# Row scaling and plain transposes in the norms of a transformer kernel, with split work, bank reads and product order changed at the stage borders

## The chip, the core and the metric

The kernel runs on one core of a Trainium2 chip. The metric is the device time of one execution in microseconds. TensorE multiplies, VectorE (DVE), ScalarE (ACT) and GpSimd (POOL) work on tiles, and SyncE (SP) issues the loads. TensorE writes its results to PSUM, which has eight banks of 512 float32 columns; all other tiles lie in SBUF, 128 rows each.

## What is computed

512 tokens of width 1024 in float32 go through two blocks. Cut to what matters here:

```python
# first block, layers i = 0 (nsa) and 1 (swa); mod = silu(c) @ ada_w[i] + ada_b[i] -> sh1, sc1, g1, sh2, sc2, g2
h = modulate(rms_norm(x, norm_g[i, 0]), sh1, sc1)
y = nsa_mixer(h, ...) if i == 0 else swa_sink_mixer(h, ...)
x = x + (1 + g1) * rms_norm(y, norm_g[i, 1])
h = modulate(rms_norm(x, norm_g[i, 2]), sh2, sc2)
x = x + (1 + g2) * rms_norm(squared_relu_mlp(h, ...), norm_g[i, 3])
# second block
x = x + hybrid_mixer(rms_norm_2(x, norm_mix_w), ...)
x = x + memory_cross_attention(rms_norm_2(x, norm_xattn_w), rms_norm_2(mem, norm_mem_w), ...)
x = x + conv_ffn(rms_norm_2(x, norm_ffn_w), ...)
return rms_norm_2(x, norm_final_w)
```

rms_norm divides each token's row by the root of its mean square and multiplies each column by a gain; modulate multiplies by 1 + scale and adds shift.

## The kernel before

The program is one straight run of stages: nsa, mlp0, swa, mlp1, hybrid, cross, ffn. `x` holds the residual as four tiles of 128 tokens by 1024 columns. What a stage multiplies, `h`, lies the other way round: eight chunks of 128 columns by 512 tokens, each as a high part `hH` and a low part `hL`, so that three products of reduced precision (`mm3`, L124 to L126: high by high, low by high, high by low) stand for one of float32. Weights come in tiles of 512 KB: `wload` loads `st`, ScalarE writes the high part `wh` (L95), and VectorE, or GpSimd where a table says so, writes the low part `wl` (L96). Loads are issued in program order; there are three `st` tiles and five pairs of `wh` and `wl`, and `extra` draws some pairs from another pool.

At a border between stages the last products of the old stage give rows of `y`, by two token tiles and then one and one. VectorE adds them up and multiplies by the gain (L914, or L916 and L918 in the mlps), ScalarE sums squares (L284), `rcol` makes the reciprocal root `rc_r` in four instructions on one column (L275 to L278), L926 adds the rows to `x`, and the same again gives the `rc_r` of the next norm. Then `norm_T` makes `h`: it builds a diagonal matrix of `rc_r` (L291) for each token tile, multiplies each 128 x 128 block of `x` by it on TensorE (L298), which turns the block round and scales it in one, and evacuates the bank: gain and shift into a tile `nt` (L308 on ScalarE and L310 on VectorE, in turn by chunk, so that both read one bank), then the split into `hH` (L95) and `hL` (L96). A norm without a shift (memory, hybrid, cross, ffn) goes from the bank at once to `hH` (L303, ScalarE) and `hL` (L304, VectorE). Behind the border the first weights of the new stage are multiplied with tokens 0 to 255 first, weight by weight, since these are ready first, and then with tokens 256 to 511: `project_halves` in the mlps with seven weights, `project` with `keep=4` in swa, hybrid, cross and ffn. The second half runs over the eight chunks `k` outside and the weights inside, so all its banks end together, each followed by its `evac`.

Besides this, `ada` jobs (L331: a load of 512 KB and one VectorE row that multiplies and sums) make the modulation of the first block; `wload` takes one from a queue for each weight, until the queue is empty. `mem_keys` (128 x 256 products, eight weights) and `mem_values` (eight weights) are work of the cross stage that is put into the borders behind mlp0 and mlp1. A scheduler with a timing model of its own orders the instructions of all engines; each engine then runs its list in order.

Of the kernel before, what the change touches and what calls it, by code (L numbers as in the profile page):

```python
# [21 lines left out]
NB = 'AVAVAVAV'  # L22
# [16 lines left out]
KG, KG4 = (4, 5, 6), (3,)  # L39
# [6 lines left out]
def body(nc, tc, A, out):  # L46
# [114 lines left out]
    def project(srcs, h, evac, keep=0, nk=8, on_pool=()):  # L161
        full = slice(0, 512)
        if keep:
            ws, banks = [], []
            for i in range(keep):
                ws.append(wload(srcs[i], eng=G if i in KG4 else V))
                banks.append(mm())
            for i in range(keep):
                mm3(banks[i][:, HALVES[0]], chunk_terms(ws[i], h, HALVES[0], range(nk)))
            for k in range(nk):  # L170
                for i in range(keep):
                    c = HALVES[1]
                    w = ws[i]
                    mm3(banks[i][:, c], [(kc(w[0], k), kc(w[1], k), h[0][k][:, c], h[1][k][:, c])], start=k == 0,
                        stop=k == nk - 1)
# [110 lines left out]
    def norm_T(xs, Rs, h, c, a, b=None):  # L286

        ds, w = [], 128 * len(xs)
        for r in Rs:
            d = tmp("diag", [128, 128], bufs=4)  # L290
            V.tensor_scalar(d, ident, r, None, op0=OP.mult)  # L291
            ds.append(d)
        nb = 512 // w
        for m0 in range(0, 8, nb):
            o = mm("t")
            for u in range(nb):
                for i, x in enumerate(xs):
                    T.matmul(o[:, u * w + i * 128:u * w + i * 128 + 128], kc(x, m0 + u), ds[i], start=True, stop=True)  # L298
            for u in range(nb):
                m = m0 + u  # L300
                hh, hl, v, g = h[0][m][:, c], h[1][m][:, c], kc(o, u, w), a[:, m:m + 1]
                if b is None:
                    S.activation(hh, v, AF.Copy, scale=g)  # L303
                    V.scalar_tensor_tensor(hl, v, g, f(hh), op0=OP.mult, op1=OP.subtract)  # L304
                else:
                    t = tmp("nt", [128, 256], bufs=3)[:, :w]
                    if NB[m] == "A":
                        S.activation(t, v, AF.Identity, bias=b[:, m:m + 1], scale=g)  # L308
                    else:
                        V.tensor_scalar(t, v, g, b[:, m:m + 1], op0=OP.mult, op1=OP.add)  # L310
                    split(hh, hl, t)
# [1294 lines left out]
```

## Time and profile before

| | |
|---|---|
| median of 3 runs | 2126.13 us (2123.41 to 2127.01) |
| profiled execution | 2125.28 us, its span 2123.2 us |
| TensorE busy | 2035.6 us, 96% of the span |
| VectorE busy | 1161.2 us, 55% |
| ScalarE busy | 905.3 us, 43% |
| GpSimd busy | 306.4 us, 14% |
| mean granted clock of TensorE | 0.975 |
| chain that ended last | TensorE 86%, VectorE 6%, ScalarE 3%, DMA 3% |

A matmul's length in the profile contains its way through the array, so that neighbours overlap; the pace is the distance from start to start. The chain of the last line is followed back from the end: at each step to what released the instruction. A wait is put down to the engine whose signal came last.

### The profile page before, as it was taken

The numbers are of one execution on the slowest core, as the hardware profiler recorded it, in microseconds if no ns is written. First come the engines' busy times: TensorE is split into PE (matmuls) and PEld (weight loads), VectorE is DVE, ScalarE is ACT, GpSimd is POOL, SyncE is SP. The second block draws the span as 40 slices with busy tenths as digits, with TensorE's granted clock in tenths as the row PEclk, the third lists the DMA queues.
The fourth block names the chain that finished last, engine by engine and source line by source line (L and its number), as shares of the span: only waits on it lengthen the run. The fifth ranks groups of instructions, "written<-read, shape, count | busy, mean of one in ns | idle before, by whom it ended". The sixth has DMA issues, their size and how long they took to land.

```text
span 2123.2 us, 27619 instructions
## 1 busy us (share of the span) xinstructions
PE 2035.6 (96%) x10326; PEld 1666.9 (79%) x10326; DVE 1161.2 (55%) x2322; ACT 905.3 (43%) x1740; POOL 306.4 (14%) x243
## 2 busy tenths in 40 slices
PE   8989999979999999799899999999999999999998
PEld 7766565778888888667788888878888888888886
DVE  7778776455556547584632333465635445445354
ACT  5356565443423236364633232453545444324233
POOL 0401121021201114310121020132010000001000
PEclk8989999999999999899899999999999999999999
DMA  7765331235557534340123233332323122323321
GB/s 292 215 211 149 96 111 48 89 130 203 183 190 228 157 111 142 88 112 30 61 99 94 94 99 99 109 105 84 100 70 109 61 82 80 99 91 98 99 93 57
DMA packets 80855, 247.79 MB, mean 117 GB/s; under 512 B 13137, under 2 KB 16145, under 8 KB 80722
## 3 DMA queue, kind: packets, MB, share of 16 engines
q1 hardware_dynamic: 77618, 240.86, 35.7%
q0 software_dynamic: 1248, 2.59, 0.5%
q10 hardware_dynamic: 1856, 2.59, 0.5%
q8 instruction: 81, 1.33, 0.3%
q14 instruction: 52, 0.43, 0.1%
HBM read 222.47 MB, written 5.77 MB: 107 GB/s over the span
## 4 chain that ended last, share of the span: by engine, by line
PE 86%; DVE 6%; ACT 3%; DMA 3%; issue 2%; ACTq 0%; SPq 0%; DVEq 0%; POOL 0%
PE mm L124 18%; PE mm L126 18%; PE mm L125 18%; PE o L124 4%; PE o L125 4%; PE o L126 4%; PE o L748 3%; PE t L433 3%; PE t L298 2%; DMA ad<-in_ada_w_dram 2%; PE t L124 2%; PE t L125 2%; PE t L126 2%; PE mm L732 1%; ACT wh L95 1%
## 5 line engine op out<-in xcount | busy, mean ns | idle before, releaser
L96 DVE TENSOR_TENSOR wl<-st,wh 128x1024 fp32r<-128x1024 f32 x273 | 341.2, 1254 | 455.2 <-ACT wh L95 454.6
L95 ACT ACTIVATE wh<-st 128x1024 fp32r<-128x1024 f32 x307 | 320.8, 1053 | 554.4 <-PE mm L125 248.2
L124 PE MATMUL mm<-hH,wh 128*128 128x512 f32 (+1 forms) x1456 | 523.4, 361 | 25.7 <-ACT wh L95 14.6
L125 PE MATMUL mm<-hL,wh 128*128 128x512 f32 (+1 forms) x1456 | 522.8, 359 | 0.0
L126 PE MATMUL mm<-hH,wl 128*128 128x512 f32 (+1 forms) x1456 | 521.8, 359 | 0.0
L124 PEld LDWEIGHTS mm<-hH,wh 128*128 128x128 f32 x1456 | 279.7, 193 | 66.5 <-ACT wh L95 19.5
L125 PEld LDWEIGHTS mm<-hL,wh 128*128 128x128 f32 x1456 | 280.0, 192 | 39.5 <-issue 1.1
L126 PEld LDWEIGHTS mm<-hH,wl 128*128 128x128 f32 x1456 | 278.9, 192 | 39.0 <-issue 0.2
L957 POOL TENSOR_TENSOR relu<-relu 128x512 f32<-128x512 f32 (+1 forms) x78 | 104.0, 1339 | 580.3 <-ACT relu L956 492.1
L124 PE MATMUL mm<-wh,aH 128*128 128x512 f32 x444 | 173.9, 393 | 3.9 <-ACT aH L95 3.9
L125 PE MATMUL mm<-wl,aH 128*128 128x512 f32 x444 | 174.2, 392 | 0.0
L126 PE MATMUL mm<-wh,aL 128*128 128x512 f32 x444 | 171.9, 392 | 0.0
L331 DVE SCALAR_TENSOR_TENSOR ad<-ad,cs 128x1024 f32<-128x1024 f32 x90 | 116.0, 1293 | 49.1 <-DMA ad<-in_ada_w_dram 48.6
L96 POOL TENSOR_TENSOR wl<-st,wh 128x1024 fp32r<-128x1024 f32 x32 | 78.1, 2455 | 424.6 <-ACT wh L95 420.7
L124 PE MATMUL o<-wh,aH 128*128 128x512 f32 x284 | 113.1, 398 | 4.8 <-DVE y L914 4.8
L125 PE MATMUL o<-wl,aH 128*128 128x512 f32 x284 | 113.0, 398 | 0.0
L126 PE MATMUL o<-wh,aL 128*128 128x512 f32 x284 | 112.2, 395 | 0.0
L124 PEld LDWEIGHTS mm<-wh,aH 128*128 128x128 f32 x444 | 83.5, 188 | 22.2 <-ACT aH L95 4.1
L126 PEld LDWEIGHTS mm<-wh,aL 128*128 128x128 f32 x444 | 83.6, 188 | 18.1
L125 PEld LDWEIGHTS mm<-wl,aH 128*128 128x128 f32 x444 | 83.5, 188 | 17.8
L433 PEld LDWEIGHTS t<-pack,P 128*128 128x128 f32 x436 | 47.1, 141 | 54.9 <-issue 49.9
L737 ACT ACTIVATE P<-P,m 128x128 f32<-128x128 f32 (+3 forms) x128 | 70.9, 556 | 28.3 <-DVE m L735 26.8
(417 smaller groups left out, 3260.0 us busy)
## 6 DMA issues: line engine op xcount, KB each, us to landing
ad<-in_ada_w_dram SPq DMA_DIRECT2D x90, 512.0 KB, 4.4
st<-in_w_up_dram SPq DMA_DIRECT2D x64, 512.0 KB, 3.6
st<-in_w_down_dram SPq DMA_DIRECT2D x64, 512.0 KB, 3.5
st<-in_w_fup_dram SPq DMA_DIRECT2D x44, 512.0 KB, 3.5
st<-in_w_fdown_dram SPq DMA_DIRECT2D x22, 512.0 KB, 3.5
st<-in_w_nsa_dram SPq DMA_DIRECT2D x16, 512.0 KB, 8.0
st<-in_w_hyb_dram SPq DMA_DIRECT2D x12, 512.0 KB, 3.6
st<-in_w_swa_dram SPq DMA_DIRECT2D x10, 512.0 KB, 3.9
```

Of the source, the lines that this page charges most:

```text
L95: S.activation(h, src, AF.Copy)
L96: eng.tensor_tensor(l, src, f(h), op=OP.subtract)
L124: T.matmul(o, ah, bh, start=start and i == 0, stop=False, **kw)
L125: T.matmul(o, ah, bl, start=False, stop=False, **kw)
L126: T.matmul(o, al, bh, start=False, stop=stop and i == n - 1, **kw)
L298: T.matmul(o[:, u * w + i * 128:u * w + i * 128 + 128], kc(x, m0 + u), ds[i], start=True, stop=True)
L331: V.scalar_tensor_tensor(w, w, 1.0, cs, op0=OP.mult, op1=OP.mult, accum_out=mod[:, j:j + 1])
L433: T.transpose(o, i, ident[:n, :n] if n < 128 else ident)
L732: T.matmul(s, kc(hq[0], qb), KK[a][:, g, :n], start=True, stop=False)
L737: S.activation(pq, pq, AF.Exp, bias=m[:, qb:qb + 1], scale=-1.0, accum_out=d[:, qb:qb + 1])
L748: T.matmul(o[64 * u:64 * u + 64], vs[u], ps_[u], start=start, stop=stop, skip_group_check=True)
L957: G.tensor_tensor(r, r, r, op=OP.mult)
```

## The change

`norm_T` first multiplies the rows: VectorE columns 0 to 511 (new L293), ScalarE columns 512 to 1023 (L294), into the `y` tile, into new tiles `xn`, or for the memory in place. TensorE then transposes the blocks plainly (L437). Each bank is evacuated by one engine, in turn by bank, and a norm without a shift takes the same way through `nt`. `late_order` lets the second half of a border's projection run over chunks 0 to 3 for all weights, then over chunks 4 to 7 weight by weight. The 26 low parts that GpSimd wrote (weights 4, 5, 6 of both mlps, weight 3 of four stages, all 16 of the memory) are VectorE's; six of swa's q projection stay with GpSimd. While `project_halves` loads, no ada job is taken. One or two of the first weights' pairs come from the stage's pool. The rows of the final gain are made before the last output rows, no longer at the beginning of ffn.

```diff
-NB = 'AVAVAVAV'
+NB = 'AVAV'
-KG, KG4 = (4, 5, 6), (3,)
+    def late_order(nk, n):
+        return ([(k, i) for k in range(nk // 2) for i in range(n)]
+                + [(k, i) for i in range(n) for k in range(nk // 2, nk)])
     def project_halves(srcs, h, evac, extra, nk=8):
-        ws = [wload(srcs[i], eng=G if i in KG else V, extra=None if i < 4 else (extra, n - 4)) for i in range(n)]
+        bg_on[0] = False
+        ws = [wload(srcs[i], extra=None if i < 4 else (extra, n - 4)) for i in range(n)]
+        bg_on[0] = True
...
-            steps = [(k, i) for k in range(nk) for i in range(n)]
-            if hi == 0:
-                steps.sort(key=lambda s: s[1])
+            steps = late_order(nk, n) if hi else [(k, i) for i in range(n) for k in range(nk)]
...
-    def project(srcs, h, evac, keep=0, nk=8, on_pool=()):
+    def project(srcs, h, evac, keep=0, nk=8, on_pool=(), extra=None):
-                ws.append(wload(srcs[i], eng=G if i in KG4 else V))
+                ws.append(wload(srcs[i], extra=extra if extra and i >= keep - extra[1] else None))
-            for k in range(nk):
-                for i in range(keep):
+            for k, i in late_order(nk, keep):
...
-    def norm_T(xs, Rs, h, c, a, b=None):
-        ds, w = [], 128 * len(xs)
-        for r in Rs:
-            d = tmp("diag", [128, 128], bufs=4)
-            V.tensor_scalar(d, ident, r, None, op0=OP.mult)
-            ds.append(d)
+    def norm_T(xs, Rs, to, h, c, a, b=None):
+        w = 128 * len(xs)
+        for x, r, t in zip(xs, Rs, to):
+            V.tensor_scalar(t[:, :512], x[:, :512], r, None, op0=OP.mult)
+            S.activation(t[:, 512:], x[:, 512:], AF.Copy, scale=r)
...
-                for i, x in enumerate(xs):
-                    T.matmul(o[:, u * w + i * 128:u * w + i * 128 + 128], kc(x, m0 + u), ds[i], start=True, stop=True)
+                for i, t in enumerate(to):
+                    transpose(o[:, u * w + i * 128:u * w + i * 128 + 128], kc(t, m0 + u))
+            on = NB[m0 // nb]
...
-                if b is None:
-                    S.activation(hh, v, AF.Copy, scale=g)
-                    V.scalar_tensor_tensor(hl, v, g, f(hh), op0=OP.mult, op1=OP.subtract)
...
+                t = tmp("nt", [128, 256], bufs=4)[:, :w]
+                if on == "A":
+                    if b is None:
+                        S.activation(t, v, AF.Copy, scale=g)
...
+                elif b is None:
+                    V.tensor_scalar(t, v, g, None, op0=OP.mult)
...
     def mem_keys(p, mh):
-            w = wload(A["w_mk"][m], eng=G)
+            w = wload(A["w_mk"][m])
...
-                wh, wl = wload(A["w_mv"][nh * 4 + j], eng=G)
+                wh, wl = wload(A["w_mv"][nh * 4 + j])
...
-        project([A["w_xq"][i] for i in range(8)], h, ev, keep=4)
+        project([A["w_xq"][i] for i in range(8)], h, ev, keep=4, extra=(p, 1))
...
-            fw = along_rows(nw["final"], tmp("along", [128, 1024], bufs=1))
+            fw = tmp("along", [128, 1024], bufs=1)
...
-            ffn(h, p, x, finish)
+            ffn(h, p, x, finish, lambda: along_rows(nw["final"], fw))
```

Three places show how the instructions move. The new program's lines are shifted by a few: L96 of before is L95 there, L275 is L278, L331 is L335, L926 is L930.

On VectorE at the border from nsa to mlp0, while the norm's last rows are evacuated (`nt`, `hL`), before:

```order
L331 SCALAR_TENSOR_TENSOR ad,mod<-ad,cs 128x1024
L291 TENSOR_SCALAR diag<-pack,rc_r 128x128
L310 TENSOR_SCALAR nt<-t,coef_1281,mod 128x128
L96 TENSOR_TENSOR hL<-nt,hH 128x128
L331 SCALAR_TENSOR_TENSOR ad,mod<-ad,cs 128x1024
L96 TENSOR_TENSOR hL<-nt,hH 128x128
L331 SCALAR_TENSOR_TENSOR ad,mod<-ad,cs 128x1024 x2
L310 TENSOR_SCALAR nt<-t,coef_1281,mod 128x128
```

and after:

```order
L293 TENSOR_SCALAR y<-x,rc_r 128x512
L95 TENSOR_TENSOR hL<-nt,hH 128x128 x2
L314 TENSOR_SCALAR nt<-t,coef_1281,mod 128x128 x2
L95 TENSOR_TENSOR hL<-nt,hH 128x128 x2
L314 TENSOR_SCALAR nt<-t,coef_1281,mod 128x128 x2
L95 TENSOR_TENSOR hL<-nt,hH 128x128 x4
L95 TENSOR_TENSOR aL<-relu,aH 128x256 x2
L95 TENSOR_TENSOR hL<-nt,hH 128x128
```

The ada rows are gone from among the evacuations: seven in this border before, none now; the last seven of the queue stand at the end of mlp0.

On VectorE at the border from mlp0 to swa, the instructions that lead to the first diagonal, before:

```order
L276 SCALAR_TENSOR_TENSOR rc_s<-rc_r 128x1
L277 SCALAR_TENSOR_TENSOR rc_s<-ss,rc_s 128x1
L278 SCALAR_TENSOR_TENSOR rc_r<-rc_s,rc_r 128x1
L926 SCALAR_TENSOR_TENSOR x<-y,rc_r,x 128x512 x2
L897 TENSOR_TENSOR ss<-ss 128x1 x2
L275 RECIPROCAL rc_r<-rc_s 128x1
L276 SCALAR_TENSOR_TENSOR rc_s<-rc_r 128x1
L277 SCALAR_TENSOR_TENSOR rc_s<-ss,rc_s 128x1
L918 TENSOR_TENSOR y<-y,along 128x512
L897 TENSOR_TENSOR ss<-ss 128x1
L278 SCALAR_TENSOR_TENSOR rc_r<-rc_s,rc_r 128x1
L291 TENSOR_SCALAR diag<-pack,rc_r 128x128
```

and after, a little ahead of the first scaling:

```order
L930 SCALAR_TENSOR_TENSOR x<-y,rc_r,x 128x512 x2
L95 TENSOR_TENSOR wl<-st,wh 128x1024 x2
L920 TENSOR_TENSOR y<-y,o 128x512
L95 TENSOR_TENSOR wl<-st,wh 128x1024
L920 TENSOR_TENSOR y<-y,t 128x512
L922 TENSOR_TENSOR y<-y,along 128x512
L901 TENSOR_TENSOR ss<-ss 128x1
L920 TENSOR_TENSOR y<-y,t 128x512
L901 TENSOR_TENSOR ss<-ss 128x1
L95 TENSOR_TENSOR wl<-st,wh 128x1024
```

Four low parts of weights of `mem_keys`, which GpSimd wrote before, and two ada rows a little further up now stand in VectorE's list ahead of the first scaling; three more stand between it and the second. At the border from mlp1 to hybrid it is four and one (low parts of `mem_values`), and no ada rows. On TensorE the first transposes of the norm stand 68 products behind the old stage's last at both borders (93 and 57 before), the second group 57 and 10 further on (19 and 3 before).

On TensorE at the end of the second half of ffn's first projection (banks `mm_15035` to `mm_15056`, weights `wh_15030` to `wh_15051`), before:

```order
L124 MATMUL mm_15035<-hH_14588,wh_15030 128x256
L125 MATMUL mm_15035<-hL_14596,wh_15030 128x256
L126 MATMUL mm_15035<-hH_14588,wl_15031 128x256
L124 MATMUL mm_15042<-hH_14588,wh_15037 128x256
L125 MATMUL mm_15042<-hL_14596,wh_15037 128x256
L126 MATMUL mm_15042<-hH_14588,wl_15038 128x256
L124 MATMUL mm_15049<-hH_14588,wh_15044 128x256
L125 MATMUL mm_15049<-hL_14596,wh_15044 128x256
L126 MATMUL mm_15049<-hH_14588,wl_15045 128x256
L124 MATMUL mm_15056<-hH_14588,wh_15051 128x256
L125 MATMUL mm_15056<-hL_14596,wh_15051 128x256
L126 MATMUL mm_15056<-hH_14588,wl_15052 128x256
```

and after (the last bank is `mm_15212`):

```order
L125 MATMUL mm_15205<-hH_14704,wl_15201 128x256
L123 MATMUL mm_15212<-hH_14701,wh_15207 128x256
L124 MATMUL mm_15212<-hL_14709,wh_15207 128x256
L125 MATMUL mm_15212<-hH_14701,wl_15208 128x256
L123 MATMUL mm_15212<-hH_14702,wh_15207 128x256
L124 MATMUL mm_15212<-hL_14710,wh_15207 128x256
L125 MATMUL mm_15212<-hH_14702,wl_15208 128x256
L123 MATMUL mm_15212<-hH_14703,wh_15207 128x256
```

Chunk by chunk through the four banks becomes bank by bank through chunks 4 to 7: the first bank's last product stands 36 instructions ahead of the last bank's last one, not 9.

## Rows read from the trace of the kernel before

**Rows 1.** The page, its first part: busy time, share of the span and instructions of each engine.

```profile
PE 2035.6 (96%) x10326; PEld 1666.9 (79%) x10326; DVE 1161.2 (55%) x2322; ACT 905.3 (43%) x1740; POOL 306.4 (14%) x243
```

**Rows 2.** The waits of TensorE over the whole span: who waited for whom, us in total, times, longest.

```profile
PE mm L124 <- ACT wh L95: 14.6, 4, 10.1
PE t L298 <- DVE diag L291: 9.9, 4, 3.7
PE mm L124 <- ACT vf L1089: 6.4, 1, 6.4
...
PE mm L124 <- DVE fu L1369: 3.8, 1, 3.8
...
PE mm L124 <- DVE xql L1344: 1.8, 1, 1.8
```

**Rows 3.** The order of time on TensorE, at two places without a wait: start, length to the end of the last, instruction, count. A product by a diagonal (L298) is two instructions for one block of 128x128, a plain transpose (L433) is one.

```profile
1433.33 1.05 PE L298 MATMUL t<-diag,x 128*128 128x128 f32 x8
1434.13 0.48 PE L126 MATMUL mm<-wh,mL 128*128 128x512 f32 x1
...
129.20 0.66 PE L433 MATMUL t<-pack,P 128*128 128x128 f32 x4
129.61 0.47 PE L125 MATMUL mm<-hL,wh 128*128 128x512 f32 x1
```

**Rows 4.** Groups of instructions by line and shape on VectorE, then GpSimd, then ScalarE: count, busy us, mean ns of one, idle time before.

```profile
L96 DVE TENSOR_TENSOR wl<-st,wh 128x1024 fp32r<-128x1024 f32 x272 | 340.5, 1256 | 454.6 <-ACT wh L95 454.0
L331 DVE SCALAR_TENSOR_TENSOR ad<-ad,cs 128x1024 f32<-128x1024 f32 x90 | 116.0, 1293 | 49.1 <-DMA ad<-in_ada_w_dram 48.6
...
L532 DVE TENSOR_SCALAR P<-P,d 128x512 f32<-128x512 f32 x32 | 17.8, 556 | 0.0
...
L291 DVE TENSOR_SCALAR diag<-pack,rc_r 128x128 f32<-128x128 f32 x28 | 7.8, 284 | 0.4
...
L96 POOL TENSOR_TENSOR wl<-st,wh 128x1024 fp32r<-128x1024 f32 x32 | 78.1, 2455 | 424.6 <-ACT wh L95 420.7 <-DVE rc_r L275 4.0
...
L303 ACT ACTIVATE hH<-t,pack 128x256 fp32r<-128x256 f32 x32 | 14.5, 471 | 20.3 <-DVE hL L304 10.5 <-PE t L298 8.8 <-PE o L125 0.9
```

**Rows 5.** The border from nsa to mlp0 in order of time: TensorE, then ScalarE, then VectorE (in brackets the idle time before and what ended it).

```profile
455.27 0.58 PE L124 MATMUL mm<-hH,wh 128*128 128x256 f32 x1 [10.15 <-ACT wh L95]
...
454.17 2.93 ACT L95 ACTIVATE wh<-st 128x1024 fp32r<-128x1024 f32 x3
...
449.24 1.63 DVE L331 SCALAR_TENSOR_TENSOR ad<-ad,cs 128x1024 f32<-128x1024 f32 x1
```

**Rows 6.** The border from mlp0 to swa in order of time: TensorE, then VectorE, then GpSimd.

```profile
816.98 0.71 PE L298 MATMUL t<-diag,x 128*128 128x128 f32 x4 [2.22 <-DVE diag L291]
...
822.98 2.93 PE L298 MATMUL t<-diag,x 128*128 128x128 f32 x12 [3.01 <-DVE diag L291]
...
801.54 2.77 DVE L918 TENSOR_TENSOR y<-y,along 128x512 f32<-128x512 f32 x1
...
806.23 1.93 DVE L276 SCALAR_TENSOR_TENSOR rc_s<-rc_r 128x1 f32<-128x1 f32 x1
...
810.49 3.64 DVE L926 SCALAR_TENSOR_TENSOR x<-y,rc_r,x 128x512 f32<-128x512 f32 x2
...
817.60 2.12 DVE L918 TENSOR_TENSOR y<-y,along 128x512 f32<-128x512 f32 x1 [0.68 <-ACT relu L284]
...
819.64 2.30 DVE L897 TENSOR_TENSOR ss<-ss 128x1 f32<-128x1 f32 x1
...
805.73 2.41 POOL L96 TENSOR_TENSOR wl<-st,wh 128x1024 fp32r<-128x1024 f32 x1 [1.98 <-DVE rc_r L275]
```

**Rows 7.** The border from mlp1 to hybrid in order of time: TensorE, then VectorE.

```profile
1415.05 0.39 PE L125 MATMUL mm<-wl,mH 128*128 128x512 f32 x1
1415.28 0.39 PE L126 MATMUL mm<-wh,mL 128*128 128x512 f32 x1
1416.64 0.71 PE L298 MATMUL t<-diag,x 128*128 128x128 f32 x4 [0.97 <-DVE diag L291]
...
1400.67 2.77 DVE L918 TENSOR_TENSOR y<-y,along 128x512 f32<-128x512 f32 x1
...
1416.90 2.05 DVE L276 SCALAR_TENSOR_TENSOR rc_s<-rc_r 128x1 f32<-128x1 f32 x2
...
1418.92 2.33 DVE L277 SCALAR_TENSOR_TENSOR rc_s<-ss,rc_s 128x1 f32<-128x1 f32 x2
```

**Rows 8.** Stretches behind four borders: us from and to, length, busy time of TensorE and instructions, granted clock (1.00 is full speed), DMA share, GB/s.

```profile
450.10:460.30 10.20, 3.94 (x16) 0.50 0.15 44
822.10:829.00 6.90, 6.03 (x28) 0.51 0.58 173
869.90:876.80 6.90, 5.16 (x12) 0.51 0.72 193
...
1419.50:1426.30 6.80, 4.55 (x17) 0.50 0.54 157
```

**Rows 9.** TensorE where the second half of the first projection of swa ends: the last two products of 256 columns, and the next one.

```profile
864.87 0.28 PE L125 MATMUL mm<-hL,wh 128*128 128x256 f32 x1
864.99 0.28 PE L126 MATMUL mm<-hH,wl 128*128 128x256 f32 x1
871.64 0.77 PE L124 MATMUL mm<-hH,wh 128*128 128x512 f32 x1 [6.37 <-ACT vf L1089]
```

More of the change, by code (lines that the diff above doesn't have):

```diff
@@ L169, in project @@
                 mm3(banks[i][:, HALVES[0]], chunk_terms(ws[i], h, HALVES[0], range(nk)))
-            for k in range(nk):
-                for i in range(keep):
[L172 to L175, printed above, removed]
+            c = HALVES[1]
+            for k, i in late_order(nk, keep):
+                w = ws[i]
+                mm3(banks[i][:, c], [(kc(w[0], k), kc(w[1], k), h[0][k][:, c], h[1][k][:, c])], start=k == 0,
+                    stop=k == nk - 1)
             for i in range(keep):
@@ L301, in norm_T @@
                 hh, hl, v, g = h[0][m][:, c], h[1][m][:, c], kc(o, u, w), a[:, m:m + 1]
-                if b is None:
-                    S.activation(hh, v, AF.Copy, scale=g)
-                    V.scalar_tensor_tensor(hl, v, g, f(hh), op0=OP.mult, op1=OP.subtract)
-                else:
[L306 to L311, printed above, removed]
+                t = tmp("nt", [128, 256], bufs=4)[:, :w]
+                if on == "A":
+                    if b is None:
+                        S.activation(t, v, AF.Copy, scale=g)
+                    else:
+                        S.activation(t, v, AF.Identity, bias=b[:, m:m + 1], scale=g)
+                elif b is None:
+                    V.tensor_scalar(t, v, g, None, op0=OP.mult)
+                else:
+                    V.tensor_scalar(t, v, g, b[:, m:m + 1], op0=OP.mult, op1=OP.add)
+                split(hh, hl, t)
     def along_rows(col, t):
@@ L379, in mem_norm @@
             rs.append(rcol(ss[:, :1], 1))
-        norm_T(ts, rs, mh, slice(0, 256), nw["mem"])
+        norm_T(ts, rs, ts, mh, slice(0, 256), nw["mem"])
     def mem_keys(p, mh):
         for m in range(8):
-            w = wload(A["w_mk"][m], eng=G)
+            w = wload(A["w_mk"][m])
             b = mm(cols=256)
@@ L927, in done @@
                     mean_sq(x[:, tb, c], s2[-1][:, n:n + 1])
-            norm_T([x[:, tb] for tb in tbs], [total(s) for s in s2], h, cols_of(tbs), an(), bn())
+            norm_T([x[:, tb] for tb in tbs], [total(s) for s in s2], [y[:, tb] for tb in tbs], h, cols_of(tbs), an(), bn())
         how(src, a, nk, evac, done)
@@ L1096, in swa @@
         w = [A["w_swa"][i] for i in range(10)]
-        project(w[:4], h, ev, keep=SK)
+        project(w[:4], h, ev, keep=SK, extra=(p, 1))
         prepare(0)
@@ L1261, in hybrid @@
         w = A["w_hyb"]
-        project([w[i] for i in range(4)], h, pooling, keep=4)
+        project([w[i] for i in range(4)], h, pooling, keep=4, extra=(p, 1))
         gl = gen()
@@ L1350, in ev, with ffn @@
                 attend(i // 2)
-        project([A["w_xq"][i] for i in range(8)], h, ev, keep=4)
+        project([A["w_xq"][i] for i in range(8)], h, ev, keep=4, extra=(p, 1))
     GROUPS = ((0, 8), (8, 8), (16, 6))
-    def ffn(h, p, x, then):
+    def ffn(h, p, x, then, ready):
         cw = p.tile([128, 3, 44], F32, name="cw", tag="cw")
@@ L1378, in ev @@
                     al.append(ll)
-            project([A["w_fup"][2 * f0 + i] for i in range(2 * n)], h, ev, keep=4 if f0 == 0 else 0)
+            project([A["w_fup"][2 * f0 + i] for i in range(2 * n)], h, ev, keep=4 if f0 == 0 else 0, extra=(p, 2))
             def src(n, j, f0=f0):
@@ L1388, in ffn @@
             else:
+                ready()
                 x_last(src, (ah, al), n, x, then)
@@ L1399, in to_h @@
         def to_h(hn, w):
-            return lambda tbs, rs: norm_T([x[:, tb] for tb in tbs], rs, hn, cols_of(tbs), w)
+            return lambda tbs, rs: norm_T([x[:, tb] for tb in tbs], rs, [tmp("xn", [128, 1024], bufs=4) for _ in tbs],
+                                          hn, cols_of(tbs), w)
         def out_of(name):
```

## The prediction

> **What bounds the kernel now.** Read the busy time of the engines first [rows 1]: TensorE is busy for 96% of the span, VectorE for 55%. So two things can move the time: less work on TensorE, or shorter waits of TensorE. The waits come second [rows 2]: they stand at the borders between stages, where a norm has to be finished on VectorE and ScalarE before there is anything to multiply. The largest groups are 14.6 us on the weight split of ScalarE (10.1 in one piece), 9.9 on the diagonals of VectorE, 6.4 on one evacuation, 3.8 and 1.8 on two more. Third come the stretches behind such waits [rows 8]: for 6.8 to 10.2 us the granted clock is 0.50 or 0.51, the lower level of 1.2 GHz, so a wait is paid a second time. Last, each border in order of time [rows 5 to 7, 9] tells what ends the wait.
>
> **The change part by part.** Sums are made against the profiled execution, 2125.3 us (span 2123.2), which stands 0.9 us below the median of the runs.
>
> *Transposes.* Six norms of 32 blocks and two memory norms of 16 make 224 blocks. Eight instructions of products by a diagonal, four blocks, take from 1433.33 to the next start at 1434.13, 0.80 us or 0.20 a block; four transposes take from 129.20 to 129.61, 0.10 a block [rows 3]. Lengths less the tail of the last give nearly the same. 224 x 0.10 = 22.4 us less work on TensorE, and that engine is the bound: **-22**. Bounds: -26 (0.115 a block, if the diagonals run at 0.112 an instruction, as the lengths allow), and -10 where the saved time only lengthens waits at the borders that still wait. The Trainium skill speaks against this: its page "TensorE: Matmul & The Clock Gate", section "Part 4: PE-mode transpose", gives about 275 ns for a 128x128 transpose in a kernel's context; paid in full, that would be an estimated 224 x (0.275 - 0.20) = 17 us more instead of 22 less. The trace disagrees: four of them end within 0.66 us and the next instruction starts after 0.41 [rows 3], so they overlap, and I take the pace.
>
> *Scaling instead of diagonals.* On VectorE 0.284 us for a diagonal becomes 0.556 for half a row block [rows 4], with ScalarE doing the other half beside it. 0.27 us more on the chain of each of 28 scalings; only the ones that TensorE waits for count, and they are in the sums of the borders. A norm without a shift (hybrid, cross, ffn and the memory) now goes through an extra tile, three operations instead of two; one more operation of about 0.47 [rows 4] ahead of the first product of three stages and the memory: **+2** (0 to +4). One engine for each bank instead of two in turn moves the same work: 0.
>
> *Border nsa to mlp0.* TensorE waits 10.15 us until ScalarE has the weight splits that stand behind the norm's rows; on VectorE an ada row of 1.63 us (mean 1.29) stands in the midst of these [rows 4, 5]. The order shows seven ada rows in this stretch, none after. The last three of them lie where the norm waits for VectorE, 3 x 1.29 = 3.9: **-4** (0 to -8; the splits of weights 4 to 6, now 3 x 1.256 on VectorE, come behind the norm and take less than TensorE's 24 products per weight). The seven rows reappear at the end of mlp0, three of them in the next border.
>
> *Border mlp0 to swa, the norm.* Five VectorE instructions take about 2 us too long each: an operation on one column takes 1.93 and another 2.30 us, and the first ends just as the GpSimd split begun at 805.73 ends [rows 6]. About 6 us of that is ahead of the first diagonal, 10 ahead of the second. All of it goes with the GpSimd splits. But the order puts four splits and two ada rows ahead of the first scaling, three more splits ahead of the second: 4 x 1.256 + 2 x 1.293 + 0.27 - 6 = 1.9 us later, and 7 x 1.256 + 2.6 + 0.3 - 10 = 1.7 later. TensorE comes to its first transposes after 68 products instead of 93, 25 x 0.12 = 3 us sooner, so the wait of 2.22 grows to about 7; it has 57 products instead of 19 before the second, so the wait of 3.01 goes. In all 5.2 becomes 7, with the half clock as before [rows 8]: **+1** (-4 to +6).
>
> *The same border, the first projection.* After the last product of 256 columns at 864.99 TensorE waits 6.37 us for a bank, then runs 6.9 us at half clock [rows 8, 9]. Products are 0.12 apart; the new order ends bank 0 36 products ahead of the last instead of 9, 27 x 0.12 = 3.2 us sooner. Its evacuation starts so much sooner: -3.2, and half of the 3.4 us that the half clock costs, -1.7: **-5** (-2 to -9.8). What is late next is the evacuation's own chain.
>
> *Border mlp1 to hybrid.* The same stretched instructions, 10 us [rows 7]. Four splits stand ahead of the first scaling, 5.0 + 0.3 - 6 = 0.7 us sooner; a fifth before the second, 6.3 + 0.3 - 10 = 3.4 sooner. TensorE arrives later, with 11 more products of 0.23 ahead of the first transposes [rows 7] and seven more before the second. Both waits (0.97 and 3.7 [rows 2, 7]) fall, and the half clock of 6.8 us, worth 3.4, with them: -8. Then only 18 products lie before the next stage instead of 35, so some 3 us come back as a wait for the norm's low halves: **-4.5** (0 to -8).
>
> *Later borders.* At swa to mlp1 the order of the norm is as before: 0 (-2 to +2). The second halves of cross and ffn end bank 0 sooner by the same 3.2 us, against waits of 1.8 and 3.8 [rows 2]: **-2** (0 to -3) and **-3** (-2 to -5.5). Moving the final gain's rows to the end of ffn hides under its products; taking the extra weight tiles from the stage's pool only frees loads early: 0 each, or 1 us where the cover is gone.
>
> **Sum:** -22 + 2 - 4 + 1 - 5 - 4.5 + 0 - 2 - 3 = -37.5, or 2125.3 - 37.5 = 2087.8, **2088 us**.
>
> **The rivals.**
> *The saved TensorE time is swallowed.* If VectorE and ScalarE set the length of the borders, faster transposes only end in a longer wait. Against it: half of the blocks lie among products, as at 1433.33 [rows 3]. For it: the other half is preceded by a wait. Then -10 instead of -22, and the clock stays low where I have it rise (+5): 2088 + 12 + 5 = 2105.
> *Better than the sum.* Every half-clock stretch behind a wait that shrinks goes: the four in [rows 8] cost (10.2 + 6.9 + 6.9 + 6.8)/2 = 15 us, of which the sum takes back 5; and transposes at -26: 2088 - 10 - 4 = 2074.
> *VectorE becomes the bound (the other side).* 26 splits of 1.256 (32.7 us), 28 longer scalings (7.6) and 7 ada rows of 1.29 (9.1) are moved onto or along VectorE's queue, 49 us, and behind them wait the rows of the norms. If TensorE has no products to cover them, they count in full, the transposes' gain is swallowed whole and only the bank and ada terms (-14) stay: 2125 + 49 - 14 = 2160. It decides where VectorE's work from the last rows of the old stage to the second scaling is longer than TensorE's products in it; by the sums above it is so at mlp0's end by some 5 us and not at mlp1's. Against it: VectorE is idle 45% of the span [rows 1], and a split costs it 1.256 us against the 2 us of a stretch.
> *A transpose costs its whole length.* Four with the tail take 0.66 [rows 3], 0.165 a block: 224 x (0.20 - 0.165) = 8 saved, 2102. One after the other without overlap each would take about 0.27 (0.66 less three paces of 0.13), 224 x (0.27 - 0.20) = 16 us lost instead of 22 saved: 2088 + 38 = 2126, no change. Against both: the next start behind four is 0.41 away, not 0.66 or 1.08. The 275 ns of the Trainium skill's page, above, are of this second kind.
>
> **How the numbers follow.** My forecast 2088: 0.52. Swallowed, or a dearer transpose (2102 to 2105): 0.20. Better (2074): 0.15. No change, by transposes that don't overlap or a VectorE bound at one border alone: 0.05. VectorE as the bound (2160): 0.08. This kernel's measurement can tell some 0.2%, 4 us, from no change. Faster by more than that 0.87, within it 0.05, slower 0.08. The range holds the first three and the bounds of the border terms: the low end is the better case less 7 for the bank waits going to their good bounds (-9.8 and -5.5), 2067; the high end the swallowed case with the norm border behind mlp0 at its bad bound (+5) and no gain at nsa's end (+4), 2114.
>
> **What would show it.** Products by diagonals gone, and transposes about 0.10 us apart at the borders; if 0.2, the first term is wrong. VectorE's one-column operations back at 0.15 us. TensorE's wait at the first transposes behind mlp0 about 7 us and gone behind mlp1; the bank wait behind swa's first projection about 3 us; the wait behind ffn's first near 0. Total waits of TensorE clearly above those of before would show VectorE as the bound. The busy time of TensorE should fall by the transposes and the clock terms, some 25 us; if it falls and the time doesn't, the saving was swallowed.

## The result, and the profile after

The changed kernel takes 2070.14 us (median of 4 runs, 2068.01 to 2075.52) against 2124.77 before (4 runs). The ratio is 0.9747, 95% interval 0.9725 to 0.9770. The forecast was 2088 in a range of 2067 to 2114: the direction and the range hold, the time close to the range's lower end, and the gain is 54.6 us instead of 37. The profiled execution has 2070.11 us and a span of 2068.3. Two executions far outside the others, one of the kernel with `vf` apart (2416 us, mean granted clock 0.764) and one of the kernel before on the same chip (4761 us), are left out of every time and ratio below.

The first part of the page after, and the granted clock in 40 slices (tenths):

```profile
PE 2002.1 (97%) x10102; PEld 1632.4 (79%) x10102; DVE 1176.3 (57%) x2388; ACT 924.8 (45%) x1808; POOL 244.7 (12%) x217
...
PEclk8989999999999999999899999999999999999999
```

Against [rows 1], TensorE is busy 33.5 us less, and 54.9 us of span went, so 21.4 us of its idle time went too. VectorE rose by 15 us and is nowhere near full. The mean granted clock rose from 0.975 to 0.979; the share missing to full clock, times the span, fell from 53 to 43 us.

TensorE's waits after (who waited for whom, us, times, longest):

```profile
PE mm L123 <- ACT wh L94: 10.6, 2, 5.5
PE mm L1064 <- DVE m L1066: 5.0, 6, 2.5
PE o L123 <- DVE y L918: 4.8, 1, 4.8
...
PE mm L123 <- ACT vf L1093: 3.2, 1, 3.2
...
PE mm L123 <- ACT xP L1322: 2.2, 1, 2.2
...
PE t L437 <- DVE xn L293: 1.1, 1, 1.1
...
PE t L437 <- DVE y L293: 0.2, 1, 0.2
```

Beside [rows 2]: the diagonals' 9.9 us have become 0.2 and 1.1 on scaled rows, the weight splits' 14.6 are 10.6, the evacuation's 6.4 is 3.2, and cross's 1.8 and ffn's 3.8 are gone. The waits on attention's row maxima (`m`) grew: they are 5.0 in six pieces here and were 2.7 in five before. Of the 10.6, 5.5 lie at the border from nsa to mlp0 and 5.1 at the one from swa to mlp1, where it was 3.4 before; this border comes up again below.

This table sets the start of the first product of each stage in the two profiled executions side by side, in us; the last column is what the stretch from the row above gained. Not all of it belongs to the change: the first row shows 0.8 us in nsa, which the change leaves alone.

| first product of | before | after | difference | gained since the row above |
|---|---|---|---|---|
| nsa's output | 380.6 | 381.3 | +0.8 | +0.8 |
| mlp0, whole width | 487.7 | 479.9 | -7.8 | -8.6 |
| mem_keys | 803.5 | 793.9 | -9.6 | -1.8 |
| swa | 839.0 | 819.0 | -20.0 | -10.4 |
| swa, whole width | 871.6 | 847.2 | -24.5 | -4.5 |
| swa's attention | 890.3 | 860.2 | -30.1 | -5.6 |
| mlp1 | 1035.8 | 1006.6 | -29.2 | +0.9 |
| mem_values | 1402.6 | 1370.8 | -31.8 | -2.6 |
| hybrid | 1434.4 | 1394.3 | -40.1 | -8.3 |
| cross, attention | 1641.0 | 1593.8 | -47.2 | -7.1 |
| ffn, whole width | 1773.2 | 1718.4 | -54.9 | -7.7 |
| (last product) | 2115.5 | 2060.7 | -54.8 | 0 |

The border from nsa to mlp0 in order of time on TensorE, after; it answers to [rows 5]:

```profile
441.70 0.60 PE L437 MATMUL t<-pack,y 128*128 128x128 f32 x4
447.79 0.58 PE L123 MATMUL mm<-hH,wh 128*128 128x256 f32 x1 [5.49 <-ACT wh L94]
```

The wait for the weight split is 5.49 instead of 10.15 us, 4.7 less. With 32 blocks transposed at half the price (3.2) this is 7.9 of the 8.6 in the table.

The border from mlp0 to swa after, on TensorE and then on VectorE; it answers to [rows 6]:

```profile
802.34 0.44 PE L437 MATMUL t<-pack,y 128*128 128x128 f32 x2 [0.16 <-DVE y L293]
...
809.45 0.82 PE L437 MATMUL t<-pack,y 128*128 128x128 f32 x6
810.03 0.36 PE L125 MATMUL mm<-mH,wl 128*128 128x256 f32 x1
```

```profile
784.36 1.22 DVE L335 SCALAR_TENSOR_TENSOR ad<-ad,cs 128x1024 f32<-128x1024 f32 x1 [0.77 <-DMA ad<-in_ada_w_dram]
...
785.51 0.68 DVE L920 TENSOR_TENSOR y<-y,o 128x512 f32<-128x512 f32 x1
786.95 1.23 DVE L335 SCALAR_TENSOR_TENSOR ad<-ad,cs 128x1024 f32<-128x1024 f32 x1 [0.76 <-DMA ad<-in_ada_w_dram]
...
801.80 0.48 DVE L293 TENSOR_SCALAR y<-x,rc_r 128x512 f32<-128x512 f32 x1
...
803.34 0.15 DVE L901 TENSOR_TENSOR ss<-ss 128x1 f32<-128x1 f32 x1
...
808.23 0.48 DVE L293 TENSOR_SCALAR y<-x,rc_r 128x512 f32<-128x512 f32 x1
```

Both waits are gone: the first transposes wait 0.16 us, the second group comes without any. An operation on one column takes 0.15 us again. The first row of `y` comes to VectorE at 785.51, 8.4 us ahead of the first mem_keys product (793.87 in the same trace); before, it came 3.9 ahead of that product (803.45):

```profile
799.57 0.69 DVE L916 TENSOR_TENSOR y<-y,o 128x512 f32<-128x512 f32 x1 [9.86 <-PE o L126]
```

The ada row at 786.95 waits 0.76 us for its load, in VectorE's list between two rows of `y`.

The windows of TensorE after (from and to, length, busy time and instructions, granted clock, DMA share, GB/s); they answer to [rows 8]:

```profile
441.90:452.10 10.20, 4.25 (x20) 0.76 0.18 52
794.00:819.00 25.00, 24.84 (x209) 1.00 0.73 226
847.20:854.20 7.00, 7.00 (x27) 0.80 0.67 196
...
1371.00:1398.00 27.00, 27.00 (x143) 1.00 0.56 177
```

Behind mlp0 and mlp1 the clock stays at 1.00 through the whole border. So the 10.4 us between mem_keys and swa are 5.1 of waits, 3.4 of half clock, and some 2 of transposes (18 blocks by diagonals before, 16 plain ones after). Behind nsa it is 0.76 over 10.2 us instead of 0.50. Behind swa's first projection it still falls, to 0.80 over 7 us, and here the wait is still there (TensorE, then VectorE, then GpSimd; it answers to [rows 9]):

```profile
843.67 0.28 PE L125 MATMUL mm<-hH,wl 128*128 128x256 f32 x1
847.15 0.77 PE L123 MATMUL mm<-hH,wh 128*128 128x512 f32 x1 [3.20 <-ACT vf L1093]
```

```profile
841.89 1.76 DVE L512 TENSOR_TENSOR P<-kb,sinT 64x512 f32<-64x512 f32 x1
843.58 2.83 DVE L513 TENSOR_TENSOR P<-kb,cosT 64x512 f32<-64x512 f32 x1
```

```profile
840.70 7.93 POOL L95 TENSOR_TENSOR wl<-st,wh 128x1024 fp32r<-128x1024 f32 x3 [14.71 <-ACT wh L94]
```

The wait fell from 6.37 to 3.20 us, by the 3.2 us that the earlier end of bank 0 was reckoned at. What ends it now: `vf` has to be written into the one buffer that `kb` lies in, two VectorE instructions of the rope still read `kb`, and these take 1.76 and 2.83 us while GpSimd does three weight splits of swa's q projection, which the change left there.

### The profile page after: what moved, and what is told of

It reads as the page before. It is cut to its first block, busy times and chain, and to the rows that moved or that the text cites. A ratio compares the mean times of both kernels' runs of the same rounds, so it can differ in the third digit from the quotient of the medians.

```text
span 2068.3 us, 27280 instructions
## 1 busy us (share of the span) xinstructions
PE 2002.1 (97%) x10102; PEld 1632.4 (79%) x10102; DVE 1176.3 (57%) x2388; ACT 924.8 (45%) x1808; POOL 244.7 (12%) x217
## 4 chain that ended last, share of the span: by engine, by line
PE 84%; DVE 6%; DMA 6%; ACT 2%; issue 2%; SPq 1%; ACTq 0%; DVEq 0%; POOL 0%
PE mm L123 19%; PE mm L125 19%; PE mm L124 19%; PE t L437 4%; PE o L752 3%; PE o L123 3%; PE o L124 3%; PE o L125 3%; DMA ad<-in_ada_w_dram 3%; PE t L123 2%; PE t L124 2%; PE t L125 2%; DVE wl L95 1%; DVE ad L335 1%; PE o L1042 1%
## 5 line engine op out<-in xcount | busy, mean ns | idle before, releaser
L95 DVE TENSOR_TENSOR wl<-st,wh 128x1024 fp32r<-128x1024 f32 (+1 forms) x299 | 370.1, 1242 | 447.4 <-ACT wh L94 446.0
L123 PE MATMUL mm<-hH,wh 128*128 128x512 f32 (+1 forms) x1456 | 519.4, 360 | 18.0 <-ACT wh L94 10.6
L335 DVE SCALAR_TENSOR_TENSOR ad<-ad,cs 128x1024 f32<-128x1024 f32 x90 | 114.2, 1273 | 62.1 <-DMA ad<-in_ada_w_dram 62.0
L437 PEld LDWEIGHTS t<-pack,P 128*128 128x128 f32 x436 | 47.2, 141 | 55.2 <-issue 50.3
L1379 POOL TENSOR_TENSOR fu<-fu 128x512 f32<-128x512 f32 x22 | 28.4, 1289 | 476.3 <-DVE fu L1373 288.7
L94 ACT ACTIVATE aH<-relu 128x512 fp32r<-128x512 f32 (+1 forms) x78 | 43.3, 555 | 91.9 <-POOL relu L961 91.7
```

What stands on the lines that cost most here:

```text
L94: S.activation(h, src, AF.Copy)
L95: eng.tensor_tensor(l, src, f(h), op=OP.subtract)
L123: T.matmul(o, ah, bh, start=start and i == 0, stop=False, **kw)
L335: V.scalar_tensor_tensor(w, w, 1.0, cs, op0=OP.mult, op1=OP.mult, accum_out=mod[:, j:j + 1])
L437: T.transpose(o, i, ident[:n, :n] if n < 128 else ident)
L1379: G.tensor_tensor(u, u, pend[0], op=OP.mult)
```

## The experiments

Twelve kernels ran. Times are medians on their chip and the ratios to the kernel before there; where a stage is named, its times are of the profiled executions. They ran on three chips, on which the kernel before has medians of 2124 to 2127 us, so a difference of two medians is good to some 3 us. Other stages move by some us between executions and with the scheduler's order, so the stage says more than the last microseconds of the total.

**One part taken back.** First the transposes: `norm_T` as before.

```diff
-            V.tensor_scalar(t[:, :512], x[:, :512], r, None, op0=OP.mult)
-            S.activation(t[:, 512:], x[:, 512:], AF.Copy, scale=r)
+            V.tensor_scalar(d, ident, r, None, op0=OP.mult)
...
-                    transpose(o[:, u * w + i * 128:u * w + i * 128 + 128], kc(t, m0 + u))
+                    T.matmul(o[:, u * w + i * 128:u * w + i * 128 + 128], kc(x, m0 + u), ds[i], start=True, stop=True)
```

> The change without its transposes: norm_T builds the diagonals and multiplies by them as before, banks read by two engines in turn, all other parts as in the change. Theory of the sum (each block of a norm is 0.10 us less on TensorE, and TensorE is the bound): 22 us back, 2092 us, with the waits of TensorE at the norms behind mlp0 and mlp1 near 0 as in the change. Rival (the saved time is swallowed by VectorE and ScalarE at the borders): at most 10 back, 2080.

Measured: 2092.52 us (2091.45 to 2093.56), ratio 0.9848 (0.9833 to 0.9862). 22.4 us back, the first theory's number: the saved time was not swallowed as a whole. Part of it was, at two borders. The products that wait there, with diagonals and then in the change:

```profile
451.54 0.39 PE L123 MATMUL mm<-hH,wh 128*128 128x256 f32 x1 [3.34 <-ACT wh L94]
1034.67 0.39 PE L123 MATMUL mm<-hH,wh 128*128 128x256 f32 x1 [2.26 <-ACT wh L94]
```

```profile
447.79 0.58 PE L123 MATMUL mm<-hH,wh 128*128 128x256 f32 x1 [5.49 <-ACT wh L94]
1025.11 0.58 PE L123 MATMUL mm<-hH,wh 128*128 128x256 f32 x1 [5.12 <-ACT wh L94]
```

The waits for a weight split behind nsa and behind swa are 2.2 and 2.9 us longer in the change, against 3.2 us of transposes saved at each border. Behind swa TensorE comes sooner to the split (with every transpose made twice, below, the wait is 3.0); behind nsa the wait goes with the new `norm_T` as a whole, for doubling leaves it at 5.6. Over the whole span the profiled executions agree: TensorE is busy 26.4 us less with transposes (2002.1 against 2028.5), its waits are 5.1 longer, and the span is 21.4 shorter.

The GpSimd splits back:

```diff
-            w = wload(A["w_mk"][m])
+            w = wload(A["w_mk"][m], eng=G)
-                wh, wl = wload(A["w_mv"][nh * 4 + j])
+                wh, wl = wload(A["w_mv"][nh * 4 + j], eng=G)
```

(and `eng=G` for weights 4 to 6 of the mlps and weight 3 of four stages)

> The change with the 26 low parts of weights on GpSimd again, all else as in the change. Theory (VectorE instructions stretched by about 2 us each beside GpSimd splits delay the norms behind mlp0 and mlp1, and TensorE waits for them and then runs at half clock): 12 to 20 us back, about 2086, with waits of TensorE for the scaled rows of 5 us and more at both borders. Rival (the borders are shorter because the last rows of the old stage come earlier and one after the other, and because of the order of products; the splits are hidden): within 4 us of the change, 2070 to 2074.

Measured: 2088.80 us (2081.18 to 2092.29), ratio 0.9825 (0.9803 to 0.9847), 18.7 us back. The waits of TensorE in this kernel:

```profile
PE mm L124 <- ACT wh L95: 12.8, 4, 5.5
PE t L438 <- DVE y L294: 7.9, 3, 4.3
```

7.9 us of waits for scaled rows are back (4.3 in one piece), and from mem_keys to swa's first product it takes 35.0 us as before (35.5), not 25.1, although here too the first row of `y` comes early (9.6 us ahead of mem_keys). The granted clock over these 35.0 us is 0.90. So the earlier row alone does not make this border short; the rival falls.

The order of the second half:

```diff
-        return ([(k, i) for k in range(nk // 2) for i in range(n)]
-                + [(k, i) for i in range(n) for k in range(nk // 2, nk)])
+        return [(k, i) for k in range(nk) for i in range(n)]
```

> The change with the second half of a border's projection chunk by chunk through all weights again (the first weights' order as before). Theory of the sum: bank waits of about 3 us more behind swa's and ffn's first projection and 2 behind cross's, with half clock behind them: 7 to 10 us back, 2079. Rival (the evacuation's own chain sets the wait, the start of it does not matter): within 4 us of the change.

Measured: 2074.03 us (2068.71 to 2078.27), ratio 0.9752 (0.9735 to 0.9769). The interval covers the change's. The stage is clearer than the total: swa's first wait is 6.4 us again instead of 3.2. The order does that, but the total shows at most some 4 us of it. At the other two places of the forecast it does not: with the old order cross waits 0.3 us instead of the 1.8 of the kernel before, and ffn's wait of 3.8 does not come back at all. Something else in the change took these two waits away. On the kernel before, neither the new `norm_T` alone nor the moved splits alone did (1.8 and 3.8 stand in both of these runs, below); the extra weight pairs from the stage's pool were not run alone.

The ada jobs:

```diff
-        bg_on[0] = False
         ws = [wload(...) for i in range(n)]
-        bg_on[0] = True
```

> The change with ada jobs taken while project_halves loads its weights, as before. Theory of the sum: the wait of TensorE at the border from nsa to mlp0 rises from 5.7 towards 10 us, about 5 us back, 2075; the end of mlp0 loses its ada rows, which stood ahead of the first scaling without a wait behind them. Rival (the three ada rows at mlp0's end cost as much as the seven at nsa's end): within 2 us of the change.

Measured: 2064.38 us (2063.17 to 2066.23), ratio 0.9716 (0.9701 to 0.9730): about 6 us faster than the change by the medians, which neither theory said, though the two intervals just touch (the change's begins at 0.9725). Its waits:

```profile
PE mm L123 <- ACT wh L94: 15.4, 2, 10.3
```

The largest is 10.3 us, at nsa's end, so the border of the forecast behaved as forecast: mlp0's whole-width products start 7.1 us later than in the change. The time comes back in swa and after. Here are the windows from swa's first whole-width product to its output, of this kernel and then of the change:

```profile
850.80:959.40 108.60, 104.05 (x575) 1.00 0.33 87
```

```profile
847.20:961.70 114.50, 108.55 (x563) 0.94 0.32 83
```

The same stretch takes 108.6 us at full clock and 114.5 at 0.94. In this kernel the scheduler put the remaining work so that nothing waits for `vf`, and the waits on row maxima are 2.8 us instead of 5.0.

This kernel also bears on the border behind mlp0. Its first row of `y` comes 3.9 us ahead of mem_keys, as in the kernel before, but 117 products instead of 68 stand ahead of the first transposes, and from mem_keys to swa's first product it takes 24.8 us without a wait. So the earlier row is not needed for a short border either.

**What holds up swa's first projection.** Two ways to take that wait away: no GpSimd split in swa, or a buffer of its own for `vf`.

```diff
-            project([w[2 + 2 * j + k]], ..., on_pool=(0,) if k in (SG if j == 1 else SG1) else ())
+            project([w[2 + 2 * j + k]], ..., on_pool=())
```

> The change with the last six GpSimd splits (weights of swa's q projection) on VectorE too. Theory (the wait of 3.2 us behind swa's first projection is for two VectorE rope instructions that read the tile that vf overwrites, 1.76 and 2.83 us long beside GpSimd splits instead of 0.67; with it goes the half clock in swa): the wait is gone and 4 to 9 us with it, 2061 to 2066. Rival (six splits of 1.2 us on VectorE delay swa's softmax, which TensorE waits for): 0 to +5.

Measured: 2061.65 us (2053.73 to 2067.33), ratio 0.9698 (0.9663 to 0.9732). The two rope instructions in this kernel:

```profile
833.91 0.68 DVE L512 TENSOR_TENSOR P<-kb,sinT 64x512 f32<-64x512 f32 x1
834.51 0.68 DVE L513 TENSOR_TENSOR P<-kb,cosT 64x512 f32<-64x512 f32 x1
```

0.68 us each, the wait for `vf` is gone, and from swa's first product to its attention's first it takes 36.4 us, the change 41.2. From swa's first product to its output it is 134.4 against 142.7, 8.2 us less and inside the 4 to 9 of the theory. The total's interval just touches the change's.

```diff
-                vf = p.tile([128, 512], F32, name="vf", tag="kb")
+                vf = p.tile([128, 512], F32, name="vf", tag="vf")
```

> The change with a tile of its own for vf, which shares one buffer with kb, whose rope reads are still stretched. Theory (TensorE's wait behind swa's first projection is for that buffer, not for the order of the products): the wait of 3.2 us is gone and 4 to 9 us with it, 2061 to 2066. Rival (the evacuation has to wait for its bank's products anyway): within 2 us of the change, 2070.

Measured: 2070.02 us (three runs: 2068.75, 2070.02, 2077.64), ratio 0.9757 (0.9723 to 0.9792): no gain. The wait for `vf` is gone, but another has taken its place:

```profile
PE mm L1064 <- DMA hq<-rBL: 4.8, 1, 4.8
```

TensorE now waits 4.8 us for the keys and queries that the rope makes, which VectorE finishes as late as before; from swa's first product to its attention it takes 41.0 us. So the bound there is the rope on VectorE, stretched by GpSimd; the buffer was only the first place where it showed. My theory of the buffer fell, that of the stretch stands.

**A price by doubling.** Every transpose of the norms made twice:

```diff
-                    transpose(o[...], kc(t, m0 + u))
+                    for _ in range(2):
+                        transpose(o[...], kc(t, m0 + u))
```

> The change with each of the 224 transposes of the norms made twice in a row into the same place, nothing else changed. Theory of the sum (a transpose takes 0.10 us of TensorE's time and TensorE is the bound): 224 x 0.105 = 23 us more than the change, 2093. Rival (a transpose costs its whole length of 0.27): 60 more, 2130. Rival (time at the borders is VectorE's): under 10 more.

Measured: 2092.70 us (2087.31 to 2096.29), ratio 0.9844 (0.9820 to 0.9868): 22.6 us more for 224 transposes, 0.101 each. Eight of them in order of time, and what follows:

```profile
1421.62 1.03 PE L438 MATMUL t<-pack,y 128*128 128x128 f32 x8
1422.41 0.36 PE L125 MATMUL mm<-hH,wl 128*128 128x256 f32 x1
```

0.79 us from the first of eight to the next product, 0.099 each. The rival with 0.27 is out. The pace is the surer of the two figures: the first stage, which the doubling does not touch, took 6.5 us longer in the profiled execution of this kernel than in that of the change, so the close agreement of the total with 224 x 0.10 may be partly luck.

**One part alone, on the kernel before.** The new `norm_T` (scaling, transposes, banks by one engine), as in the change's diff:

> The kernel before with the new norm_T alone: rows scaled first, plain transposes, banks read by one engine each; GpSimd splits, product order and ada jobs as before. Theory of the sum: 22 us less on TensorE, some of it lost in the norms behind mlp0 and mlp1, where VectorE's stretched chain sets the end: 15 to 22 less than before, 2103 to 2110. Rival (the gain of the transposes needs the freed VectorE): 5 to 12 less.

Measured: 2098.64 us (2094.43 to 2106.80), ratio 0.9879 (0.9847 to 0.9910), some 26 to 29 us less than before, more than expected. The border from mem_keys to swa already takes 30.5 us instead of 35.5 in it, and from mlp1's mem_values to hybrid 28.7 instead of 31.9 (VectorE's instruction of 2.77 us in [rows 6], for example, takes 0.76 there).

The 26 splits moved to VectorE, as in the change's diff:

> The kernel before with the 26 low parts on VectorE instead of GpSimd, nothing else changed. Theory (stretched VectorE instructions delay the norms behind mlp0 and mlp1): both waits for the diagonals (9.9 us in all) and the half clock behind them go, 12 to 19 less than before, 2106 to 2113. Rival (the 8 splits at each of these borders are as long on VectorE as the stretches were): within 4 us of before.

Measured: 2111.04 us (2107.27 to 2111.13), ratio 0.9933 (0.9916 to 0.9950), 14 to 15 less. The waits:

```profile
PE mm L124 <- ACT wh L95: 13.1, 3, 10.8
PE mm L124 <- ACT vf L1089: 6.4, 1, 6.4
```

No wait for a diagonal is left; those at nsa's end and for `vf` stand as before. From mem_keys to swa's first product it takes 25.7 us at a granted clock of 1.00, so the moved splits alone make this border nearly as short as the change does (25.1).

The ada jobs held:

> The kernel before with ada jobs held while project_halves loads, nothing else changed. Theory of the sum, for which the change without this part speaks against: the wait at the border from nsa to mlp0 falls from 10.2 to about 6 us and the total by 4, 2121. Rival (the jobs that are put off stand among the norm's rows at the end of mlp0, where VectorE's chain sets the end): the border gains 4 to 7 us and the one behind mlp0 loses as much or more, 2125 to 2132.

Measured: 2116.17 us (2112.12 to 2121.18, 10 runs), ratio 0.9958 (0.9946 to 0.9971), 9 to 10 us less; the profiled execution, one of the slower of the ten, has 2121. The waits in it:

```profile
PE t L300 <- DVE diag L293: 11.3, 3, 6.6
PE mm L124 <- ACT wh L95: 8.1, 4, 3.3
```

The largest wait for a weight split fell from 10.1 to 3.3 us, and the waits for diagonals rose from 9.9 to 11.3 (6.6 in one piece, behind mlp0): first as the sum said, then as the rival said, and the first is larger here.

**An evacuation in two operations** where there is no shift:

```diff
+                if b is None:
+                    S.activation(hh, v, AF.Copy, scale=g)
+                    V.scalar_tensor_tensor(hl, v, g, f(hh), op0=OP.mult, op1=OP.subtract)
+                    continue
```

> The change with a norm without a shift evacuated in two operations as before (ScalarE writes the high part from the bank, VectorE the low part from the same bank), transposes and all else as in the change. Theory of the sum (one operation less ahead of the first products of hybrid, cross and ffn): 2 us less, 2068. Rival (two engines reading one bank in turn hold each other up): 0 to +4.

Measured: 2074.85 us (2071.75 to 2076.65), ratio 0.9761 (0.9746 to 0.9776): not faster, perhaps some us slower. The +2 of the sum for the third operation was not seen, but this run does not isolate it. The wait for `vf` is absent here, and two waits stand in it that the change lacks, 2.8 us ahead of cross's attention and 5.7 at the border from cross to ffn, where a transpose waits for VectorE's low part:

```profile
1699.21 0.69 PE L436 MATMUL t<-pack,xn 128*128 128x128 f32 x2 [5.67 <-DVE hL L307]
```

So the price of either way of evacuating stays open.

**Both faster runs together**, ada jobs taken and no GpSimd split in swa:

> The change with ada jobs taken during project_halves again and with no GpSimd splits in swa: the two runs that were faster than the change, together. Theory (both gain by the same thing, a swa stage without a wait and half clock behind its first projection): no more than the better of the two, 2060 to 2065. Rival (they are separate gains of 6 and 8 us): 2055.

Measured: 2068.04 us (2064.06 to 2068.88), ratio 0.9727 (0.9712 to 0.9741), not below the better of the two. They don't add, as the first theory said. The stages show why: from swa's first product to its output it takes 133.8 us with the ada jobs back, 134.4 without GpSimd splits and 134.4 with both (142.7 in the change), the same gain once, and with the ada jobs back the wait of 10.3 us at nsa's end is paid as well. The fastest by its median is the change with swa's splits on VectorE, 0.9698; its interval and that of 0.9716 for the ada jobs overlap, and both just touch the change's.

## Why the prediction was right, and where it was off

- *Bound and place of the waits.* Right: TensorE's own work and the borders. Nearly all the gain lies in the borders' rows of the table; the mlps' and ffn's long stretches moved by 0 to 2.6 us.
- *Transposes, -22.* Right in mechanism and price: 22.4 back without them, 22.6 more with twice as many. Behind nsa and swa part of it came back as longer waits, which the sum did not have there. The Trainium skill's 275 ns for one transpose (page "TensorE: Matmul & The Clock Gate", section "Part 4: PE-mode transpose") agrees with the length of one in this trace, 0.27 us; the doubled kernel shows that a further one costs 0.10 us in a row of them.
- *Border nsa to mlp0, -4.* Right: the wait fell from 10.15 to 5.49.
- *The norm behind mlp0, +1.* This is the step that was furthest off. It had the first wait grow from 2.22 to about 7, since TensorE comes to its transposes after 68 products instead of 93. The wait is 0.16, and the stretch from mem_keys to swa gained 10.4 us where the sum had a loss of 1 and the transposes' share of some 2. I had dated VectorE's chain from the end of the old stage. In the new list TensorE ends one of the last banks earlier, so the first row of `y` came 8.4 instead of 3.9 us ahead of mem_keys; 4.5 us of the error is that. The chain from that row to the first scaling took 16.3 us where my sum gave 17.1 + 1.9 = 19.0; that is 2.7 more. With both waits gone the half clock, 6.9 us long, went as well (3.4). This division holds for the list of the change only. What the border needs is VectorE freed of GpSimd's splits: with them back it takes 35.0 us in spite of the earlier row, with the ada jobs back 24.8 without it, and on the kernel before the moved splits alone bring it to 25.7. The scheduler's lists differ in these runs (44, 117 and 83 products stand ahead of the transposes, against 68), so how much each of the two dates is worth is not shown by them.
- *The bank behind swa's first projection, -5.* Right: 6.37 to 3.20, by 27 products of 0.12, and the clock behind it at 0.80 instead of 0.51. The further -5.6 up to swa's attention was not in the sum. TensorE waited there for the keys and queries that come back through a DMA, which the list of its waits in the kernel before shows and that of the change no longer has; the prediction left this term out:

```profile
PE mm L1060 <- DMA hq<-rBL: 4.7, 1, 4.7
```

Some of it came back behind, in the waits on row maxima (2.7 to 5.0).

- *The norm behind mlp1, -4.5.* Right: 8.3 with its transposes, 7.7 reckoned; both waits went and the clock stayed full.
- *swa to mlp1, 0.* The waits for weight splits grew there from 3.4 to 5.1 us. From swa's attention to mem_values the table gains 1.7, where the transposes of this norm and of the memory's second alone are 4.8 and more waits on row maxima stand against them.
- *Cross and ffn, -2 and -3.* With transposes 5.2 and 6.2 reckoned; the stages gained 7.1 and 7.7 in the table, hybrid's own stretch included. The waits went, but not by the reason given: they stay away with the old order of the products, so the amount was right by luck. What took them away stays open; the extra weight pairs, which the sum put at 0, are the part that no run took alone. *A third operation, +2*: not seen, and not isolated.
- *The rivals.* The swallowed gain is refuted as a whole by the transposes taken back and doubled; it happened at two borders, about 5 us of 22. The bound VectorE is refuted by its 57% and by the moved splits, which alone make the kernel before 14 to 15 us faster. The measured 2070 lies nearer to "better than the sum" (2074) than to my 2088. Its mechanism came half true: of the four half-clock stretches the two behind mlp0 and mlp1 went, those behind nsa and in swa rose to 0.76 and 0.80, and the transposes gave 22, not 26.
- *The ada jobs.* Holding them alone gains 9 to 10 us, and in the change their return makes it some 6 faster, with intervals that touch. The border of nsa does what was forecast in both. The gain from their return does not come from a cost of the moved jobs that I could show (the border behind mlp0 waits for none of them in the change but 0.76 us); it goes with a swa stage without a wait and half clock, which differs by the scheduler's order. Why the order came out so stays open.

## What to carry to other kernels

A time saved on the engine that bounds is a safe term where no wait stands right behind it: price it by the distance between starts at a place without waits, confirm it by doubling the instruction, and look at the next wait, which can take it back (here some 5 of 22 us). A border is a race of two chains, and both have to be dated: not only how long VectorE's list is but when its first input is ready in the new order, and how many products cover it. A wait that goes after several edits is not yet the work of the edit that was meant for it: take that edit back and see whether the wait returns (it did in swa, not in ffn). Work on GpSimd beside VectorE is not free work: look for one-column operations of 2 us before leaving a split there, and if one stretch is taken away, look for the next chain that is stretched (here the rope).

## What was not expected of the hardware

- From swa's first whole-width product to its output the granted clock was 0.94 on the mean in the change and 1.00 with the ada jobs back, and the stretch 5.9 us longer with the same products (114.5 against 108.6). That the wait of 3.2 us ahead of it is the cause is not shown: the kernel with the two-operation evacuation has no such wait and takes 114.2 us at 0.96, and the waits inside the stretch differ as well (5.0 against 2.8 us on row maxima).
- Between executions of one program on one chip the total moved by up to 14 us (2053.73 to 2067.33 without swa's GpSimd splits), more than the 6.5 us between runs of the kernel before (2121.80 to 2128.30 on the chip of the run with `vf` apart); the first stage alone, which no experiment changed, started its output between 377.3 and 387.8 us.
